# Shift and scale of a modulation as TensorE products with one moving column, in a hybrid state-space and attention layer

## The chip, the core and the metric

The kernel runs on one core of a Trainium2 chip. The metric is the device time of one execution in microseconds (us). The kernel computes in float32; its large products use the float32r form of TensorE on operands that are split in two parts.

## The reference

Only the beginning of the layer matters here. The conditioning vector `c` (1024 numbers) makes a shift, a scale and a gate for each of the 1024 channels; the tokens (2048 rows of 1024 channels) are normalized, scaled and shifted, and projected by `w_in`:

```python
c_act = jax.nn.silu(c)
mod = c_act @ w_ada[l] + b_ada[l]                # (1, 3072), w_ada is 1024 x 3072
shift, scale, gate = jnp.split(mod, 3, axis=-1)
u = _layer_norm(h) * (1.0 + scale[:, None, :]) + shift[:, None, :]
proj = u @ w_in[l]                               # 1024 x 5128: x_ssm first, then z, q, k, v, ...
```

After that come a state-space branch, an attention branch, a gated merge, an output projection and a last layer norm.

## The kernel before

All instructions are issued through small wrappers (`pe`, `dve`, `act`, `pool`, `sp`), so that the profile puts nearly all of them on line L209, and groups are told apart by the names of tiles. The order of the instructions is decided when the kernel is built: every part of the work is a Python generator (a stream), and `Model.merge` emits from the first stream whose next step would not wait by a rough clock of the engines, whose costs are in `Model.cost`. At run time each engine works its own list strictly in that order.

The first stage, called the prologue here, handles the first window of 512 tokens. Its streams are these.

- `modulation` forms shift and scale in eight steps `kt`, each for 128 channels of both. A step's weights come in a tile `wada` of 128x8x256 (two transfers, 1 MB), from a ring of four such tiles; step `kt` lets the load for `kt + 4` go. With `cact` = silu(c) as eight columns, VectorE (DVE) makes a weighted sum `acc` of six of the eight blocks (one product, five multiply-adds, 128x256 each); ScalarE (ACT) weights the other two into `pr`, and GpSimd (POOL) adds those.
- `modulation_columns` sums `acc` and `pr` over the partitions: TensorE (PE) multiplies them by the identity into a bank `bg`, 128x128 at a time, DVE reduces the 256 columns to two and adds the bias; the result is two columns of `mods`.
- `normalized` and `modulated` make the normalized tokens `xt`, transpose them on PE into a bank `pt` (four 128x128 transposes for each `kt`), and ACT makes `u` (float32) and `uh` (its rounding) from `pt` and `mods`. `low_parts` makes `ul` = `u` - `uh`. There are two `pt` banks.
- `first_weights` splits the rows `wk` of `w_in` into `hi` and `lo`.
- `phase_1a` multiplies: for each `kt` and each of four column tiles, three products of 128x512 (`uh,hi`, `ul,hi`, `uh,lo`) into banks `pp`; 96 for the first window. Then come early keys (tiles `wke`) and the next windows.

Of the kernel before, what the change touches and what calls it, by code (L numbers as in the profile page):

```python
# [16 lines left out]
S = 2048  # L17
D = 1024
NW = 4          # token windows of 512
WT = 512  # L20
KD = D // 128
NG = 32         # state-space groups
GH = 16         # channels of a group
CL = 8          # tokens of a chunk
NCH = S // CL   # chunks
CW = WT // CL   # chunks of a window
# [10 lines left out]
PKN = 163       # of a group: Bbar 16 | swapped 16 | C 16 | swapped 16 | tables 64 | powers 19 | A^7..A^0 16  # L37
# [4 lines left out]
class Model:  # L42
    """A rough clock of the engines, by which the order of emission is chosen (it computes no data)."""

    # from the end of an instruction to the start, on another engine (or the same), of one that needs it
# [34 lines left out]
    def deps(self, e, kw):  # L80
        """When the operands are there for engine e (whose own accesses are in order)."""
        rd, wt = self.aps(kw)
        r = 0.0
        for n in rd:
            if n in self.wr:
                end, by = self.wr[n]
                r = max(r, end + self.lat(e, by))
            for h in self.held:
                if n in h[2]:           # (a transfer that is still to come)
                    r = max(r, max(h[0] + 1100, self.t["sp"] + 1100, self.t["dma"]) + 1700)  # L90
# [8 lines left out]
    def cost(self, e, op, kw):  # L99
# [4 lines left out]
        if e == "pe":  # L104
            if op == "transpose":
                return n * 0.835
            if kw["rhs"].dtype == F32R:
                return max(n, 2) * (0.4167 if n >= 256 else 1.667)
            return max(n * 1.667, 60.0)
# [24 lines left out]
    def run(self, e, op, kw):  # L134
# [11 lines left out]
        for n in wt:  # L146
            # parts of a tile that transfers fill do not wait for each other
# [3 lines left out]
    def settle(self, rd, wt, dma=False):  # L151
        """Emit what is held and has to come before a read of rd and a write of wt (transfers may fill parts of a
        tile in any order)."""
# [14 lines left out]
    def merge(self, streams):  # L168
        """Emit from the first stream whose next step would not wait; streams come in order of rank."""
# [27 lines left out]
class Engine:  # L197
    """An engine whose instructions the model sees."""
# [14 lines left out]
    def when(self, **kw):  # L213
        """When an instruction with these operands could start."""
# [3 lines left out]
    def soon(self, op, /, **kw):  # L218
        """A stream's step: the instruction, emitted once it would not wait."""
        yield self.when(**kw)  # L220
        getattr(self, op)(**kw)

    def later(self, op, /, **kw):
        """The instruction, emitted once its operands are there (the streams go on meanwhile)."""
# [6 lines left out]
def hybrid_layer(ctx: ExitStack, tc: tile.TileContext, x, c, w_ada, b_ada, w_in, b_f, lam_re, lam_im,  # L231
# [32 lines left out]
    def pround(o, i):  # L264
        """Pool's copy into float32r (its rounding)."""
# [19 lines left out]
    # maskb[q, k] = 0 where k <= q, NEG elsewhere  # L285
# [4 lines left out]
    # ------------------------------------------------------------------ phase 1: input projection  # L290
    esl = ExitStack()               # left: until the projection is done
# [11 lines left out]
    def ps_tile(n=[0]):  # L303
        """One of four banks, which attention later has for scores (three) and outputs."""
# [7 lines left out]
    def bg_tile(n=None):  # L312
        if n is not None and n % 4 > 1:         # (the banks of the transposes, once attention is done)
# [6 lines left out]
    def bank():  # L320
        """Whichever of the two banks of bg_tile is free."""
# [12 lines left out]
    def split_wide(raw, n):  # L334
        """A stream that splits a chunk of weights; the tiles are there at once."""
# [8 lines left out]
    def rstd_of(p, mv, n):  # L344
        """1 / sqrt(var + eps) of the variances mv[:, :, 1]."""
# [21 lines left out]
    def until(f):  # L367
        """A condition to wait on, whatever the time."""
        return lambda: 0.0 if f() else None

    def modulation():
        """shift | 1 + scale of silu(c) @ w_ada + b_ada, as columns, 128 channels at a time."""
# [3 lines left out]
        act.activation(out=one, in_=ident[:, 0:1], func=AF.Sqrt)    # (its table is there when the layer norm needs it)  # L376
        dve.tensor_scalar(out=cth, in0=cth, scalar1=1.0, scalar2=0.5, op0=ALU.add, op1=ALU.mult)
        dve.tensor_mul(out=cact, in0=cact, in1=cth)
        prs = []

        def products(kt):
            wt = wts[kt]
            pr = T(adp, [128, 2, 256], F32, tag="pr", bufs=2, name="pr")
            for i in range(2):
                yield from act.soon("activation", out=pr[:, i], in_=wt[:, 6 + i], func=AF.Identity,
                                    scale=cact[:, 6 + i:7 + i])
            yield from pool.soon("tensor_add", out=pr[:, 0], in0=pr[:, 0], in1=pr[:, 1])
            prs.append(pr)

        yield until(lambda: units)  # L390
# [5 lines left out]
        yield from products(0)  # L396
        for kt in range(KD):
            wt = wts[kt]
            acc = T(adp, [128, 256], F32, tag="acc", bufs=2, name="acc")
            yield from dve.soon("tensor_scalar", out=acc, in0=wt[:, 0], scalar1=cact[:, 0:1], scalar2=None,  # L400
                                op0=ALU.mult)
            for k in range(1, 6):
                dve.scalar_tensor_tensor(out=acc, in0=wt[:, k], scalar=cact[:, k:k + 1], in1=acc, op0=ALU.mult,
                                         op1=ALU.add)
            if kt + 1 < KD:
                yield from products(kt + 1)
# [9 lines left out]
            accs.append((acc, prs.pop(0)[:, 0]))  # L416

    accs, ek = [], []

    def early_keys():  # L420
        """Two column tiles of the keys' weights, with which the first window goes on while the next one comes."""
# [7 lines left out]
    def modulation_columns():  # L429
        """Sums over the partitions, as columns."""  # L430
        m2 = mods.rearrange("p (a k) -> p a k", k=KD)
        b2 = bt.rearrange("p (a k) -> p a k", k=KD)
        for kt in range(KD):
            yield until(lambda: accs)
            ab = accs.pop(0)
            ps = bg_tile()
            yield pe.when(out=ps, a=ab[0], b=ab[1])
            for i in range(2):
                c = slice(i * 128, (i + 1) * 128)
                for j in range(2):  # L440
                    pe.matmul(out=ps[:, c], lhsT=ab[j][:, c], rhs=ident, start=(j == 0), stop=(j == 1))
            o = m2[:, 0:2, kt]
            yield from dve.soon("tensor_reduce", out=o, in_=ps[:, 0:256].rearrange("p (a b) -> p a b", b=128),
                                axis=AX.X, op=ALU.add)
            dve.tensor_add(out=o, in0=o, in1=b2[:, 0:2, kt])
            done["mods"] = kt + 1

    def column_sums(acc, n, c0):
        """mods[:, c0:] = sums of acc over its partitions, as columns, + b_ada."""
# [34 lines left out]
    def normalized():  # L484
        """Windows of tokens, less their mean and over their spread."""
# [21 lines left out]
    def modulated():  # L507
        """u = normalized * (1 + scale) + shift, channels on partitions."""
# [28 lines left out]
    def low_parts():  # L537
        """The two parts of u."""
        for n in range(32):
# [4 lines left out]
            yield from (pool if w == 0 or kt % 2 else dve).soon("tensor_sub", out=ul[w][kt], in0=ut, in1=f32(uh[w][kt]))  # L544
# [17 lines left out]
    def products_of(ps, w, hi, lo, c0):  # L562
        """A tile of columns of the projection of a window."""
# [7 lines left out]
    def store_parts(kind, m, w, ps):  # L571
        """Queries (scaled) or keys, in two parts."""
# [1218 lines left out]
```

## Time and profile before

| What | Value |
|---|---|
| three runs | 1916.01, 1917.6, 1920.11 us; median 1917.6 us |
| profiled execution: span of its trace, the only time that the page gives of it | 1913.3 us |
| PE busy (matmul) / weight loads | 96% / 82% of the span |
| DVE, ACT, POOL busy | 57%, 41%, 48% |
| DMA, mean over the span | 132 GB/s |

The span goes from the first to the last instruction on the chip; the 4.3 us between it and the median lie around it. A busy PE counts the time from a matmul's start to the modelled end of its last column, so that matmuls which follow each other overlap, and their distance from start to start, not their duration, says what each one takes.

### The profile page before, as it was taken

To read this page: it belongs to the slowest core of one execution; us is meant where nothing else is said; L and a number is where in the kernel's file an instruction comes from. 1 tells how busy PE (TensorE), PEld (TensorE's weight loads), DVE (VectorE), ACT (ScalarE), POOL (GpSimd) and SP (SyncE) were. 2 spreads that over 40 slices of the span, in tenths; PEclk is the share of its full clock that TensorE was granted. 3 is DMA by queue.
4 is the path that set the end of the run, shared out by engine and by line. 5 is a ranking of instruction groups with operands and counts; after the bars stand their busy time and mean duration, and the time that the engine had idled before them with its cause. 6 is when DMAs were issued, how large, how long until landed. Compare 5 with 4: busy or idle time off the path is not lost. (4 is left out here: it accounts for less than half of the span.)

```text
span 1913.3 us, 30538 instructions
## 1 busy us (share of the span) xinstructions
PE 1833.8 (96%) x10104; PEld 1565.5 (82%) x10104; DVE 1082.5 (57%) x2886; ACT 775.1 (41%) x1849; POOL 923.6 (48%) x1343
## 2 busy tenths in 40 slices
PE   4999999998999999999998999999999999899997
PEld 3789988886787888888887888988889888788886
DVE  8651114734555555552004777876777866567666
ACT  5441111121433444443114767876767866311110
POOL 5222111113889999995306566376543436533110
PEclk9899999998999999999998999999999999999999
DMA  9434346654333333335217365265364543744432
GB/s 302 138 86 119 94 110 183 149 133 121 101 94 105 100 105 97 105 101 138 91 50 189 98 169 140 77 183 152 113 201 131 151 137 127 260 146 136 131 123 89
DMA packets 276915, 252.37 MB, mean 132 GB/s; under 512 B 66396, under 2 KB 211828, under 8 KB 276756
## 3 DMA queue, kind: packets, MB, share of 16 engines
q1 hardware_dynamic: 276756, 250.41, 45.7%
q8 instruction: 80, 1.31, 0.3%
q14 instruction: 79, 0.65, 0.1%
HBM read 159.50 MB, written 86.63 MB: 129 GB/s over the span
## 5 line engine op out<-in xcount | busy, mean ns | idle before, releaser
L209 PE MATMUL pp<-uh,hi 128*128 128x512 f32 x1136 | 451.0, 397 | 0.0
L209 PE MATMUL pp<-uh,lo 128*128 128x512 f32 x1136 | 446.0, 393 | 0.0
L209 PE MATMUL pp<-ul,hi 128*128 128x512 f32 x1136 | 445.1, 392 | 0.0
L209 ACT ACTIVATE st<-pp 128x512 f32<-128x512 f32 (+2 forms) x168 | 93.9, 559 | 439.1 <-PE pp L209 383.4
L209 DVE TENSOR_TENSOR pl<-pt,ph 128x512 fp32r<-128x512 f32 (+1 forms) x288 | 183.3, 657 | 122.3 <-ACT ph L209 121.7
L209 PEld LDWEIGHTS pp<-uh,lo 128*128 128x128 f32 x1136 | 214.2, 189 | 46.3
L209 PEld LDWEIGHTS pp<-uh,hi 128*128 128x128 f32 x1136 | 216.4, 190 | 41.5
L209 PEld LDWEIGHTS pp<-ul,hi 128*128 128x128 f32 x1136 | 214.7, 189 | 41.9
L209 ACT ACTIVATE srow<-srow,nm 128x512 f32<-128x512 f32 (+2 forms) x320 | 207.6, 653 | 0.4 <-DVE nm L209 0.3
L209 ACT ACTIVATE ph<-pt 128x512 fp32r<-128x512 f32 (+1 forms) x288 | 159.8, 572 | 64.4 <-PE pt L209 51.6
L209 DVE CUSTOM_DVE_ANT_0 srow<-sc,fb 128x512 f32<-128x512 f32 (+3 forms) x288 | 163.0, 594 | 21.9 <-PE sc L209 21.9
L209 PE MATMUL sc<-ks,qd 128*128 128x512 f32 (+2 forms) x640 | 163.7, 381 | 7.1 <-DMA qd<-q_sc 7.1
L209 PE MATMUL pt<-ident,srow 128*128 128x128 f32 x1088 | 159.3, 275 | 8.7 <-DVE pl L209 4.7
L209 PE MATMUL acc<-ph,vs 128*128 128x256 f32 x576 | 163.0, 308 | 2.5 <-POOL ph L209 2.5
L209 POOL TENSOR_TENSOR oo<-oo 64x256 f32<-64x256 f32 x128 | 93.7, 732 | 143.0 <-ACT oo L209 140.0
L209 POOL TENSOR_SCALAR hi<-raw 128x512 fp32r<-128x512 f32 x60 | 39.9, 665 | 237.8 <-PE pp L209 191.7
L209 PEld LDWEIGHTS pt<-ident,srow 128*128 128x128 f32 x1088 | 128.4, 141 | 27.2 <-DVE pl L209 9.5
L209 PE MATMUL acc<-pl,vs 128*128 128x256 f32 x576 | 147.4, 282 | 0.5 <-DVE pl L209 0.5
L209 PE MATMUL bg<-bh,wh 128*128 128x512 f32 (+1 forms) x384 | 140.2, 365 | 5.1 <-DVE zt L209 5.1
L209 PE MATMUL bg<-bh,wl 128*128 128x512 f32 (+1 forms) x384 | 138.1, 360 | 0.0
L209 PE MATMUL bg<-bl,wh 128*128 128x512 f32 (+1 forms) x384 | 137.8, 359 | 0.0
L209 PEld LDWEIGHTS sc<-ks,qd 128*128 128x128 f32 x640 | 107.9, 193 | 24.4 <-issue 8.4
(240 smaller groups left out, 3811.3 us busy)
## 6 DMA issues: line engine op xcount, KB each, us to landing
xt<-in_x_dram SPq DMA_DIRECT2D x32, 512.0 KB, 3.7
qd<-q_sc SPq DMA_DIRECT2D x64, 256.0 KB, 5.4
raw<-in_w_in_dram SPq DMA_DIRECT2D x30, 512.0 KB, 4.5
wada<-in_w_ada_dram SPq DMA_DIRECT2D x16, 512.0 KB, 7.0
k_sc<-st SPq DMA_DIRECT2D x32, 256.0 KB, 3.3
v_sc<-st SPq DMA_DIRECT2D x32, 256.0 KB, 2.3
q_sc<-st SPq DMA_DIRECT2D x16, 512.0 KB, 3.3
gs_sc<-st SPq DMA_DIRECT2D x32, 256.0 KB, 2.3
```

Of the source, the lines that this page charges most:

```text
L209: return fn(kw["out"], 0.0) if op == "memset" else fn(**kw)
```

## The change

The weighted sums leave DVE, ACT and POOL. Each 128x128 block of a `wada` tile becomes the weights of a float32 matmul, and one column of `cact` (128x1) is the moving operand; eight such products add up in one column of the bank `bg`, so that a step `kt` is sixteen matmuls, and DVE adds the bias straight from `bg`. `modulation_columns` goes. `modulation` no longer waits until the first tokens are normalized. The model takes at least 110 ns instead of 60 for a float32 matmul, and for the first window the `ul` subtractions go to DVE, where they were on POOL. Comments and docstrings are dropped as well.

```diff
@@ class Model: cost
-            return max(n * 1.667, 60.0)
+            return max(n * 1.667, 110.0)
@@ modulation
-        prs = []
-
-        def products(kt):
-            wt = wts[kt]
-            pr = T(adp, [128, 2, 256], F32, tag="pr", bufs=2, name="pr")
-            for i in range(2):
-                yield from act.soon("activation", out=pr[:, i], in_=wt[:, 6 + i], func=AF.Identity,
-                                    scale=cact[:, 6 + i:7 + i])
-            yield from pool.soon("tensor_add", out=pr[:, 0], in0=pr[:, 0], in1=pr[:, 1])
-            prs.append(pr)
-
-        yield until(lambda: units)
         ps = bg_tile()
         yield pe.when(out=ps, in_=braw)
         pe.transpose(out=ps[:, 0:24], in_=braw, identity=ident[0:24, 0:24])
         dve.tensor_copy(out=bt, in_=ps[:, 0:24])
         dve.tensor_scalar(out=bt[:, 8:16], in0=bt[:, 8:16], scalar1=1.0, scalar2=None, op0=ALU.add)
-        yield from products(0)
+        m2 = mods.rearrange("p (a k) -> p a k", k=KD)
+        b2 = bt.rearrange("p (a k) -> p a k", k=KD)
         for kt in range(KD):
             wt = wts[kt]
-            acc = T(adp, [128, 256], F32, tag="acc", bufs=2, name="acc")
-            yield from dve.soon("tensor_scalar", out=acc, in0=wt[:, 0], scalar1=cact[:, 0:1], scalar2=None,
-                                op0=ALU.mult)
-            for k in range(1, 6):
-                dve.scalar_tensor_tensor(out=acc, in0=wt[:, k], scalar=cact[:, k:k + 1], in1=acc, op0=ALU.mult,
-                                         op1=ALU.add)
-            if kt + 1 < KD:
-                yield from products(kt + 1)
+            ps = bg_tile()
+            yield pe.when(out=ps, a=wt, b=cact)
+            for i in range(2):
+                for k in range(KD):
+                    pe.matmul(out=ps[:, i:i + 1], lhsT=wt[:, k, i * 128:(i + 1) * 128], rhs=cact[:, k:k + 1],
+                              start=(k == 0), stop=(k == KD - 1))
             if kt + 4 < KD:
                 load_ada(kt + 4)
...
-            accs.append((acc, prs.pop(0)[:, 0]))
+            yield from dve.soon("tensor_add", out=m2[:, 0:2, kt], in0=ps[:, 0:2], in1=b2[:, 0:2, kt])
+            done["mods"] = kt + 1
@@ modulation_columns (whole)
-            for i in range(2):
-                c = slice(i * 128, (i + 1) * 128)
-                for j in range(2):
-                    pe.matmul(out=ps[:, c], lhsT=ab[j][:, c], rhs=ident, start=(j == 0), stop=(j == 1))
-            o = m2[:, 0:2, kt]
-            yield from dve.soon("tensor_reduce", out=o, in_=ps[:, 0:256].rearrange("p (a b) -> p a b", b=128),
-                                axis=AX.X, op=ALU.add)
-            dve.tensor_add(out=o, in0=o, in1=b2[:, 0:2, kt])
-            done["mods"] = kt + 1
@@ low_parts
-            yield from (pool if w == 0 or kt % 2 else dve).soon("tensor_sub", out=ul[w][kt], in0=ut, in1=f32(uh[w][kt]))
+            yield from (pool if w and kt % 2 else dve).soon("tensor_sub", out=ul[w][kt], in0=ut, in1=f32(uh[w][kt]))
@@ hybrid_layer
-    M.merge([normalized(), modulation_columns(), modulation(), low_parts(), first_weights(), early_keys(), modulated(), phase_1a()])
+    M.merge([normalized(), modulation(), low_parts(), first_weights(), early_keys(), modulated(), phase_1a()])
```

PE's list changes in the prologue. Before, it begins as follows; the names are the bank, then the moving tile and the weights.

```order
L209 MATMUL bg<-ident,braw 128x24
L209 MATMUL pt<-ident,xt 128x128 x4
L209 MATMUL bg<-ident,acc 128x128
L209 MATMUL bg<-ident,pr 128x128
L209 MATMUL bg<-ident,acc 128x128
L209 MATMUL bg<-ident,pr 128x128
```

With the change it begins like this.

```order
L209 MATMUL bg<-ident,braw 128x24
L209 MATMUL bg<-cact,wada 128x1 x16
L209 MATMUL pt<-ident,xt 128x128 x8
L209 MATMUL bg<-cact,wada 128x1 x16
L209 MATMUL pt<-ident,xt 128x128 x4
L209 MATMUL pp<-uh_0_84,hi 128x512
L209 MATMUL pp<-ul_0_100,hi 128x512
L209 MATMUL pp<-uh_0_84,lo 128x512
```

A block of sixteen one-column products stands ahead of the first transposes, and a second one ahead of the first products `pp`. Further on, between two blocks, PE's list has this pattern, up to the eighth block (here from the third to the fourth).

```order
L209 MATMUL bg<-cact,wada 128x1 x16
L209 MATMUL pp<-uh_0_84,hi 128x512
L209 MATMUL pp<-ul_0_100,hi 128x512
L209 MATMUL pp<-uh_0_84,lo 128x512
L209 MATMUL pt<-ident,xt 128x128 x4
L209 MATMUL pp<-uh_0_84,hi 128x512
L209 MATMUL pp<-ul_0_100,hi 128x512
L209 MATMUL pp<-uh_0_84,lo 128x512
L209 MATMUL bg<-cact,wada 128x1 x16
```

So six `pp` products stand between two blocks, 36 of the window's 96 come before the eighth block, and 60 after it. After the first three windows of tokens the lists of all engines are the same as before but for the numbers of buffers.

On SP, which issues the transfers, the list before has these rows from the last two `wada` tiles on; `xt` are the tokens of the second window.

```order
L209 DMA wada<-in_w_ada_dram 128x8x128 x2
L209 DMA wke<-in_w_in_dram 128x8x256
L209 DMA xt<-in_x_dram 128x1024 x2
L209 DMA xt_404<-in_x_dram 128x1024
L209 DMA xt_405<-in_x_dram 128x1024
```

With the change these are the rows.

```order
L209 DMA wada<-in_w_ada_dram 128x8x128 x2
L209 DMA wk<-in_w_in_dram 128x512
L209 DMA xt<-in_x_dram 128x1024 x2
L209 DMA xt_394<-in_x_dram 128x1024
L209 DMA xt_395<-in_x_dram 128x1024
L209 DMA wke<-in_w_in_dram 128x8x256
```

The tokens of the second window go ahead of the early keys' weights; the `wada` transfers keep their places.

## Rows read from the trace of the kernel before

**Rows 1.** The page: span, and busy time of PE and of its weight loads.

```profile
span 1913.3 us, 30538 instructions
PE 1833.8 (96%) x10104; PEld 1565.5 (82%) x10104; DVE 1082.5 (57%) x2886; ACT 775.1 (41%) x1849; POOL 923.6 (48%) x1343
```

**Rows 2.** Stretches of 5 us: length, busy us (instructions) by engine, PEclk, DMA share, GB/s.

```profile
30.00:35.00 5.00, 5.00 (x27) 4.14 (x27) 4.51 (x9) 3.43 (x9) 4.09 (x5) 1.00 1.16 317
40.00:45.00 5.00, 3.30 (x21) 2.56 (x21) 4.82 (x8) 4.25 (x10) 3.68 (x4) 1.00 1.16 311
45.00:50.00 5.00, 2.56 (x10) 1.57 (x8) 4.82 (x6) 2.68 (x6) 5.00 (x7) 0.57 1.05 397
50.00:55.00 5.00, 4.18 (x15) 3.39 (x15) 4.82 (x8) 1.96 (x3) 3.39 (x3) 0.50 0.23 91
55.00:60.00 5.00, 4.27 (x17) 3.82 (x18) 3.80 (x9) 2.18 (x4) 2.25 (x2) 0.56 0.00 0
60.00:65.00 5.00, 5.00 (x23) 4.07 (x22) 4.83 (x13) 1.83 (x4) 2.10 (x2) 1.00 0.93 341
```

**Rows 3.** Groups of instructions of the first 90 us: busy us, mean ns, idle before.

```profile
L209 DVE SCALAR_TENSOR_TENSOR acc<-wada,cact,acc 128x256 f32<-128x256 f32 x40 | 30.7, 768 | 1.4
...
L209 POOL TENSOR_TENSOR ul<-u,uh 128x512 fp32r<-128x512 f32 x9 | 12.0, 1336 | 32.8 <-DVE uh L209 21.6 <-ACT uh L209 11.2
...
L209 DVE TENSOR_SCALAR acc<-wada,cact 128x256 f32<-128x256 f32 x8 | 5.7, 706 | 0.3 <-issue 0.3
...
L209 DVE TENSOR_TENSOR ul<-u,uh 128x512 fp32r<-128x512 f32 x2 | 1.3, 638 | 0.0
```

**Rows 4.** Timeline (start us, us): ACT waits for the second and the fourth `wada`.

```profile
17.20 0.91 ACT L209 ACTIVATE pr<-wada,cact 128x256 f32<-128x256 f32 x2 [0.70 <-DMA wada<-in_w_ada_dram]
...
25.86 0.91 ACT L209 ACTIVATE pr<-wada,cact 128x256 f32<-128x256 f32 x2 [1.08 <-DMA wada<-in_w_ada_dram]
```

**Rows 5.** Timeline: the eighth and last pair of columns of `mods`.

```profile
58.27 0.78 DVE L209 TENSOR_TENSOR mods<-mods,bt 128x2 f32<-128x2 f32 x1
```

**Rows 6.** Timeline of PE and its weight loads: float32 pairs, and transposes of 32 columns.

```profile
19.25 0.63 PE L209 MATMUL bg<-ident,pr 128*128 128x128 f32 x2
...
19.68 0.63 PE L209 MATMUL bg<-ident,acc 128*128 128x128 f32 x2
...
33.88 0.39 PE L209 MATMUL bg<-ident,pr 128*128 128x128 f32 x2
...
34.10 0.39 PE L209 MATMUL bg<-ident,acc 128*128 128x128 f32 x2
...
386.74 0.82 PEld L209 LDWEIGHTS pt<-ident,Qp 32*128 32x128 f32 x12 [0.35 <-issue]
```

**Rows 7.** Views by tile, weight loads: ns min/median/max, first and last start, form.

```profile
L209 PEld LDWEIGHTS bg<-ident,acc x4: 187/191/192, 33.6 to 34.1; 128*128 128x128 f32 x4
...
L209 PEld LDWEIGHTS bg<-CA,pkg x62: 92/94/96, 482.2 to 867.0; 128*16 128x16 f32 x62
...
L209 PEld LDWEIGHTS pt<-ident,Qp x21: 133/137/140, 386.7 to 391.7; 32*128 32x128 f32 x21
```

**Rows 8.** Timeline of PE: transposes, and products of the first window up to its end.

```profile
24.56 1.91 PE L209 MATMUL pt<-ident,xt 128*128 128x128 f32 x8
...
31.18 0.63 PE L209 MATMUL pp<-ul,hi 128*128 128x512 f32 x1
...
31.60 0.60 PE L209 MATMUL pp<-uh,lo 128*128 128x512 f32 x1
...
34.55 0.60 PE L209 MATMUL pt<-ident,xt 128*128 128x128 f32 x4
...
72.50 0.39 PE L209 MATMUL pp<-uh,lo 128*128 128x512 f32 x1
...
72.73 0.39 PE L209 MATMUL pp<-uh,wke 128*128 128x512 f32 x1
```

**Rows 9.** PE's groups between 13 and 59.4 us, one of the three `pp` kinds.

```profile
L209 PE MATMUL pp<-uh,hi 128*128 128x512 f32 x13 | 6.9, 529 | 0.0
```

More of the change, by code (lines that the diff above doesn't have):

```diff
@@ L415, in modulation @@
                 ek.append(T(adp, [128, KD, 256], F32R, tag="wada", bufs=4, name="wke"))
-            accs.append((acc, prs.pop(0)[:, 0]))
-    accs, ek = [], []
+            yield from dve.soon("tensor_add", out=m2[:, 0:2, kt], in0=ps[:, 0:2], in1=b2[:, 0:2, kt])
+            done["mods"] = kt + 1
+    ek = []
     def early_keys():
@@ L427, in early_keys @@
         done["ek"] = True
[L429 to L437, printed above, removed]
-            for i in range(2):
-                c = slice(i * 128, (i + 1) * 128)
-                for j in range(2):
-                    pe.matmul(out=ps[:, c], lhsT=ab[j][:, c], rhs=ident, start=(j == 0), stop=(j == 1))
-            o = m2[:, 0:2, kt]
-            yield from dve.soon("tensor_reduce", out=o, in_=ps[:, 0:256].rearrange("p (a b) -> p a b", b=128),
-                                axis=AX.X, op=ALU.add)
-            dve.tensor_add(out=o, in0=o, in1=b2[:, 0:2, kt])
-            done["mods"] = kt + 1
     def column_sums(acc, n, c0):
```

## The prediction

> **What bounds the kernel now.** I read the page first: PE is busy for 96% of the span [rows 1], so work taken from another engine pays only where PE waits. Then I cut the beginning into stretches of 5 us and looked for idle PE [rows 2]: it works 3.30 of 5 us from 40 to 45, 2.56 from 45 to 50, and from 60 on all of it. DVE is busy 4.82 of 5 us through 40 to 55, and the DMA share, 1.16 at 30 to 45, falls to nothing by 55. So the transfers had ended while DVE was still at work: DVE bounds the prologue.
>
> The groups say with what [rows 3]: 40 multiply-adds and 8 products on `wada`, 30.7 + 5.7 = 36.4 us. ACT waits for the second and the fourth `wada` at 17.20 and 25.86 us [rows 4], so a step's weights (with a `wk`) land every 4.33 us; the first pair is then there at 12.9 and, if the queue stays full, the eighth at 25.86 + 4 x 4.33 = 43.2 (estimates). The eighth pair of `mods` is ready only at 58.27 + 0.78 = 59.05 us [rows 5], 16 us later.
>
> Third, TensorE's clock. PEclk reads 1.00 at 30 to 35 [rows 2], but the rows there come in two kinds: two halves of a float32 product are 0.43 us apart from the next two at 19.25 and 0.22 at 33.88 [rows 6], a `pp` product takes 0.42 at 31.18 and 0.23 at 72.50 [rows 8]. That is 1.2 and then 2.4 GHz. By the means of 0.57 and 0.56 [rows 2] the clock falls near 45.7, after the half idle stretch, and rises near 59.4, in a stretch with PE at work for 4.27 us. The stretch before has 4.18 us of work and stays at 0.50. Work of some 4 us is thus sometimes enough and sometimes not.
>
> My yardstick is the end of the first window's 96 `pp` products, the start of the first `wke` product: 72.73 us [rows 8]. From there PE has no idle time for a long while and its later list is unchanged, so a shift of this point is a shift of the whole. When `mods` is complete, near 59.4, 13 products of each of the three kinds are done, 39 of 96 [rows 9], much as the 36 that will stand ahead of the last block: the race is for the date of `mods`. I add it to the median, 1917.6; the profiled execution's span, 1913.3 [rows 1], lies 4.3 below and moves alike.
>
> **The change part by part.** *Removed.* DVE's 36.4 us, the reductions, ACT's and POOL's part in the sums: all bought only the dates of `mods`. On PE, 64 half products of 128 columns go (each float32 matmul shows as two rows, with two weight loads).
>
> *Added.* 8 x 16 = 128 float32 matmuls with one moving column, 256 halves, each with a load of 128x128 weights. The trace has no float32 matmul with few columns. Below stand transposes with 32 columns: 12 loads in 0.82 us, of which one takes 0.137, so (0.82 - 0.137) / 11 = 0.062 us each [rows 6, 7]. Above stands the pair of 128 columns: (34.10 - 33.88) / 2 = 0.11 us a half, and 0.215 at 1.2 GHz [rows 6]. I take the upper end, since the load sets it: outside transposes a load of 128 columns takes 191 ns and one of 16 takes 94 [rows 7], 0.87 ns a column, 111 ns for 128; the transposes' loads are of the faster sort, 137 ns. One moving column leaves nothing to hide such a load behind. A block of 16 matmuls is then 32 x 0.1125 = 3.6 us at 2.4 GHz, 32 x 0.215 = 6.9 us at 1.2; eight blocks are 29 or 55 us, against 64 x 0.1125 = 7.2 us removed.
>
> *Moved.* Blocks stand in PE's list ahead of the transposes and `pp` products, and PE works strictly in order: between two blocks there are four transposes (0.11 or 0.215 us each) and six `pp` (0.23 or 0.42), so 1.8 or 3.4 us. DVE's add waits for its block, and behind it stands that step's `ul`, which needs it anyhow. `ul` on DVE takes 0.64 us where POOL took 1.34 [rows 3], hidden: DVE is now nearly empty. On SP the second window's tokens pass the early keys; those keys are used only from the yardstick on, and behind 2 MB of tokens their 1 MB takes, at the 397 GB/s of 45 to 50 [rows 2], till about 52 us (an estimate), so it is hidden. The floor of 110 ns in the model sets only the order shown.
>
> *The sum, at 1.2 GHz.* First block from 13.0 to 19.9; eight transposes to 21.6; second block to 28.5; four transposes and six `pp` to 31.9; third block to 38.8; five more rounds of 3.4 + 6.9 = 10.3 end the eighth block at 90.0; the 60 `pp` that are left, dense and at 2.4 GHz, 13.8 us: 103.8, which is 31 us later than 72.7. Each round at 2.4 GHz instead takes 5.4 and saves 4.8. No row shows what one-column matmuls do to the clock, since the array takes in one column where loads take 111 ns; I liken them to idle time, after which the clock fell at 45.7. The 3.4 us of dense work in a round may raise it now and then, as above: I give that one round of the six. 31 - 4.8 = 26, so 1917.6 + 26 = **1944 us**.
>
> **The rivals.** *The clock comes up* and stays, because PE has no gap from 13 us on. First block half at 1.2 (16 x 0.215 + 16 x 0.1125 = 5.2): 18.2; transposes 0.9; block 3.6: 22.7; transposes and `pp` 1.8, third block 3.6: 28.1; five rounds of 5.4: 55.1; then 13.8: 68.9. That is 3.8 us early, 1913.8: the edge of no change, since about 0.2% (3.8 us) is what a measurement of this kernel can tell. For it: the clock rose twice in dense work. Against it: the 4.18 us at 0.50 [rows 2]. The Trainium skill, page "TensorE: Matmul & The Clock Gate", section "Why this matters for your kernels", advises to keep TensorE continuously busy to reach its full rate; by that rule blocks without gaps would give this rival's time, and the trace agrees at 59.4 and not at 50 to 55.
>
> *Cheap loads*, the case on the faster side: a half costs the transposes' 0.062 us, a block 2.0, and the clock is up. A round of 2.0 + 1.8 is then shorter than the 4.33 between landings, the weights' arrival bounds, and the eighth block ends at 43.2 + 2.0; 13.8 more make 59.0, 13.7 us early: 1904. It decides from 0.079 us a half on ((4.33 - 1.8) / 32). Against it stand the 191 and 94 ns. The same page, section "Weight-path perf modes — Fast Weight Load (FWL) and DoubleRow", excludes float32 weights from the fast load; by it the sum keeps 0.1125, and the 191 ns agree.
>
> *Clock up in most rounds*, four or five of six: 31 - 4.5 x 4.8 = 9 us late, 1927.
>
> **How the numbers follow.** Low clock with none to three rounds up: 0.58, from 1934 to 1949, and to 1953 if the first `pp` after the last block are slow too (some 8 at 0.2 more) and the runs spread by the 2.5 us that they show. Clock up in most rounds 0.08. Clock up throughout 0.28, spread by some 4 us around 1914: 0.12 faster, 0.14 no change, 0.02 slower. Cheap loads 0.06. Most rounds up: 0.02 no change, 0.06 slower. Faster by over 0.2%: 0.12 + 0.06 = 0.18; within: 0.14 + 0.02 = 0.16; slower: 0.58 + 0.06 + 0.02 = 0.66. The range that holds 8 in 10 takes in both clocks: 1912 to 1953. That of the likeliest case alone is 1934 to 1953.
>
> **What would show it.** `bg<-cact,wada`: start to start of halves 0.11 (2.4 GHz) or 0.215 (1.2), against 0.06 in the cheap case. Granted clock: 0.5 in most stretches up to the last block; if 1.00 from 20 us on, the first rival. The eighth add into `mods` near 85 to 90 us (55 or 45 in the rivals), the first `wke` product near 99. ACT and DVE should wait for PE there, and PE for nobody: if PE waits for `uh` or `wada`, my picture of a PE-bound prologue is wrong. From then on each stretch should look as before, only later.

## The result, and the profile after

The changed kernel takes 1946.98 us (median of four executions, 1943.97 to 1947.41), the kernel before beside it 1918.86 (four, 1916.01 to 1921.13): the ratio is 1.0138, with a 95% interval of 1.0121 to 1.0154. It is slower by 28 us; the prediction was 1944, slower by 26. That closeness is partly luck: two terms were off by some 7 us each, in opposite directions, and a later set of executions of the same kernel gave 1957.8.

The page of the profile after begins as follows.

```profile
span 1945.6 us, 30824 instructions
PE 1873.8 (96%) x10296; PEld 1605.0 (82%) x10296; DVE 1050.3 (54%) x2838; ACT 767.9 (39%) x1833; POOL 907.4 (47%) x1327
```

Against [rows 1] DVE has 32 us less to do and the kernel is slower; PE has 40 us more, in 192 more rows. These are the stretches of 5 us that answer to [rows 2] (length, busy us and instructions of PE, PEld, DVE, ACT and POOL, then PEclk, DMA share, GB/s).

```profile
40.00:45.00 5.00, 5.00 (x35) 4.60 (x34) 0.45 (x2) 1.76 (x4) 0.00 (x0) 0.78 0.46 128
45.00:50.00 5.00, 5.00 (x38) 4.77 (x36) 0.41 (x1) 0.29 (x1) 1.61 (x2) 0.84 1.12 342
50.00:55.00 5.00, 5.00 (x28) 4.39 (x27) 0.86 (x2) 2.06 (x4) 1.62 (x2) 0.70 1.03 394
55.00:60.00 5.00, 5.00 (x27) 4.51 (x27) 0.85 (x2) 2.06 (x4) 0.64 (x1) 0.64 0.41 131
60.00:65.00 5.00, 5.00 (x25) 4.81 (x23) 0.00 (x0) 0.00 (x0) 1.00 (x2) 0.50 0.00 0
...
95.00:100.00 5.00, 3.16 (x18) 2.56 (x19) 3.27 (x8) 3.22 (x5) 1.27 (x1) 1.00 0.89 217
```

The picture of [rows 2] is turned round. From 40 to 60 us DVE, 4.82 of 5 us busy before in most of them, now does 0.41 to 0.86; PE, half idle before, is busy all the time up to 90 us. And yet PEclk reads 0.50 to 0.84 up to 65 us: PE is not idle there and runs at 1.2 GHz for much of the time. The timeline of PE shows where (start us, us, the row's form, xcount; a block of sixteen products is one row of x32, and the row behind it says where it ended).

```profile
13.38 6.99 PE L209 MATMUL bg<-cact,wada 128*128 128x1 f32 x32
20.23 1.95 PE L209 MATMUL pt<-ident,xt 128*128 128x128 f32 x8
...
32.10 3.83 PE L209 MATMUL bg<-cact,wada 128*128 128x1 f32 x32
35.80 0.66 PE L209 MATMUL pp<-uh,hi 128*128 128x512 f32 x1
...
39.24 3.71 PE L209 MATMUL bg<-cact,wada 128*128 128x1 f32 x32
...
60.66 6.82 PE L209 MATMUL bg<-cact,wada 128*128 128x1 f32 x32
67.34 0.77 PE L209 MATMUL pp<-uh,hi 128*128 128x512 f32 x1
...
70.90 6.82 PE L209 MATMUL bg<-cact,wada 128*128 128x1 f32 x32
77.58 0.77 PE L209 MATMUL pp<-uh,hi 128*128 128x512 f32 x1
```

The first block takes 20.23 - 13.38 = 6.85 us, or 0.214 us a half; the third 3.70, or 0.116. Four of the eight blocks (at 32.10, 39.24, 46.28 and 53.28) are of the short sort, four of the long. The rounds (a block and the transposes and products up to the next one) tell more: from one long block to the next it is 70.90 - 60.66 = 10.24 us, and from a short one to the next 39.24 - 32.10 = 7.14. The clock rose near the beginning of such a block and was down again near its end, so the block is short and little else; nearly all transposes and `pp` products between blocks stay at 1.2 GHz in either case. The view by tile gives the durations (ns, least, median, most).

```profile
L209 PEld LDWEIGHTS bg<-cact,wada x256: 187/331/337, 13.4 to 77.3; 128*128 128x128 f32 x128
L209 PE MATMUL bg<-cact,wada x256: 164/352/373, 13.4 to 77.4; 128*128 128x1 f32 x128
```

A load of 128 columns takes 187 ns at least, as in [rows 7], and 331 in the median, since most ran at 1.2 GHz. The last pair of `mods`, in DVE's timeline, comes 19 us later than in [rows 5]:

```profile
77.75 0.16 DVE L209 TENSOR_TENSOR mods<-bg,bt 128x2 f32<-128x2 f32 x1 [6.96 <-PE bg L209]
```

DVE had waited 6.96 us for PE. Behind that come the 60 `pp` products that are left, and at the end something new. These are rows of PE's timeline again, with the idle time before a row and what ended it in brackets.

```profile
82.84 0.63 PE L209 MATMUL pp<-uh,hi 128*128 128x512 f32 x1
83.27 0.60 PE L209 MATMUL pp<-ul,hi 128*128 128x512 f32 x1
...
84.18 0.39 PE L209 MATMUL pp<-ul,hi 128*128 128x512 f32 x1
84.41 0.40 PE L209 MATMUL pp<-uh,lo 128*128 128x512 f32 x1
...
94.40 0.49 PE L209 MATMUL pt<-ident,xt 128*128 128x128 f32 x3
96.41 0.76 PE L209 MATMUL pt<-ident,xt 128*128 128x128 f32 x5 [1.52 <-ACT xt L209]
97.60 0.66 PE L209 MATMUL pt<-ident,xt 128*128 128x128 f32 x4 [0.43 <-ACT u L209]
98.01 0.48 PE L209 MATMUL pp<-uh,wke 128*128 128x512 f32 x1
```

The first 14 of them, from 77.58 to 83.27, are some 0.43 us apart; the clock comes up near 83.7, and then they are 0.23 apart. Then PE stands still for 1.52 and 0.43 us for the second window's tokens, and the yardstick of the prediction, the first `wke` product, comes at 98.01; it was at 72.73 in [rows 8]. ACT's timeline says why the tokens are late.

```profile
87.20 1.23 ACT L209 ACTIVATE xt<-xt,nm,rs 128x1024 f32<-128x1024 f32 x1
92.50 0.60 ACT L209 ACTIVATE st<-pp 128x512 f32<-128x512 f32 x1 [4.07 <-PE pp L209]
92.99 1.24 ACT L209 ACTIVATE xt<-xt,nm,rs 128x1024 f32<-128x1024 f32 x1
94.12 0.59 ACT L209 ACTIVATE st<-pp 128x512 f32<-128x512 f32 x1
```

In ACT's list an eviction `st` stands between the second and the third `xt`; it waits 4.07 us for PE to finish a bank, and the third and fourth `xt` wait with it.

### The profile page after: what moved, and what is told of

Read it like the earlier page. It is cut to its first block, busy times and chain, and to the rows that moved or that the text cites. A ratio compares the mean times of both kernels' runs of the same rounds, so it can differ in the third digit from the quotient of the medians.

```text
span 1945.6 us, 30824 instructions
## 1 busy us (share of the span) xinstructions
PE 1873.8 (96%) x10296; PEld 1605.0 (82%) x10296; DVE 1050.3 (54%) x2838; ACT 767.9 (39%) x1833; POOL 907.4 (47%) x1327
```

## The experiments

Every comparison is with the kernel before, run beside it on the same chip; the experiments ran on three chips (numbers 8, 10 and 12), and that of the first result is not known. The theory: PE's blocks are priced by their weight loads, and by a clock that single moving columns leave at 1.2 GHz. The rivals: the float32 loads, or the columns, cost more in themselves; the order or the other parts of the change are to blame.

**128 columns instead of one.** The same products, with silu(c) spread over 128 equal columns.

```diff
+        cw = adp.tile([128, KD, 128], F32, name="cw")
+        dve.tensor_scalar(out=cw, in0=cact.unsqueeze(2).to_broadcast([128, KD, 128]), scalar1=1.0, scalar2=None, op0=ALU.mult)
-                    pe.matmul(out=ps[:, i:i + 1], lhsT=wt[:, k, i * 128:(i + 1) * 128], rhs=cact[:, k:k + 1],
+                    pe.matmul(out=ps[:, i * 128:(i + 1) * 128], lhsT=wt[:, k, i * 128:(i + 1) * 128], rhs=cw[:, k, :],
```

> The blocks of w_ada stay the weights, in the same 128 float32 matmuls, but the moving operand is 128 equal columns (silu(c) spread out once by VectorE) where the change has one. Theory: the price of a half is its weight load, 0.112 us at 2.4 GHz and 0.2135 at 1.2, with one column or 128; what the single column costs beyond that is the clock, which the changed kernel's trace shows at 0.50 in most stretches up to 83 us. With 128 columns the clock then comes up by the second or third block and stays; blocks take 3.6 to 3.7 us, the eighth add into mods comes near 55 us, the first wke product between 70 and 78, and the time is 1914 to 1924 us, some 25 us under the changed kernel. Rival 1: the float32 loads themselves, or the chain of halves into one bank, hold the clock down; then it stays at 0.50 as now, with 1943 to 1950 us. Rival 2: 128 columns lengthen a half (columns and load add up, near 0.165 us at 2.4 GHz); then blocks take 5.3 us even at the full clock and the time is some 12 us above the theory's, 1928 to 1936.

Measured: 1925.02 us, ratio 1.003 (1.0016 to 1.0043). These are rows of PE's timeline.

```profile
14.43 5.21 PE L211 MATMUL bg<-cw,wada 128*128 128x128 f32 x32 [1.07 <-DVE cw L211]
19.48 0.60 PE L211 MATMUL pt<-ident,xt 128*128 128x128 f32 x4
...
47.36 3.73 PE L211 MATMUL bg<-cw,wada 128*128 128x128 f32 x32
50.85 0.48 PE L211 MATMUL pp<-uh,hi 128*128 128x512 f32 x1
...
72.25 0.77 PE L211 MATMUL pt<-ident,xt 128*128 128x128 f32 x5 [1.51 <-ACT xt L211]
73.45 0.66 PE L211 MATMUL pt<-ident,xt 128*128 128x128 f32 x4 [0.43 <-ACT u L211]
73.86 0.48 PE L211 MATMUL pp<-uh,wke 128*128 128x512 f32 x1
```

With 128 times the columns a half is cheaper, not dearer: 3.49 us a block, 0.109 a half. The clock rose within the first block, near 17.5 us, and stays up through the prologue. Both rivals fall: neither the float32 loads nor the chain of halves into one bank hold the clock down, and 128 columns do not lengthen a half. What the single column cost beyond this is 1946.98 - 1925.02 = 22 us, worked out from two sets of runs; against the later, slower set of the changed kernel (below) it is 33. The time lies 1 us above what was expected; the wait for `xt` is here too, and the first block starts 1 us later for `cw`.

**One product of eight.** Each step forms its sums from `k = 0` alone; seven eighths of the sum are left out.

```diff
-                for k in range(KD):
-                    pe.matmul(out=ps[:, i:i + 1], lhsT=wt[:, k, i * 128:(i + 1) * 128], rhs=cact[:, k:k + 1],
-                              start=(k == 0), stop=(k == KD - 1))
+                pe.matmul(out=ps[:, i:i + 1], lhsT=wt[:, 0, i * 128:(i + 1) * 128], rhs=cact[:, 0:1],
+                          start=True, stop=True)
```

> Each step forms its two columns from one of the eight products only (k = 0), so seven eighths of the sum are left out and the numbers that follow are others; transfers, adds and all later work stay. TensorE's part in the modulation is then 2 matmuls a step in place of 16. Theory: the loss of the changed kernel is TensorE's time for the blocks, at a low clock; without it the arrival of the weights is the bound, the eighth add into mods comes near 45 us, the first wke product near 60, and the time is 1904 to 1910 us, faster than before by 0.4 to 0.7%. Rival: freed of the blocks, the first window runs into something else that is late (the second window's normalized tokens, for which TensorE already waited 1.52 + 0.43 us at 96 to 98 in the changed kernel, or the low clock in the gaps between arrivals); then 1913 to 1918 us, no better than before.

Measured: 1905.46 us, ratio 0.9929 (0.9911 to 0.9947). In PE's timeline the last block waits for its weights.

```profile
44.25 0.38 PE L209 MATMUL bg<-cact,wada 128*128 128x1 f32 x2 [1.31 <-DMA wada<-in_w_ada_dram]
...
53.76 0.50 PE L209 MATMUL pp<-uh,wke 128*128 128x512 f32 x1 [2.62 <-ACT wke L209]
```

So the weights are there by 44.2 us, and what stands between the changed kernel and 1905 us is PE's time for its blocks and the low clock that goes with them. At this yardstick that is 19 us less than in [rows 8]; the next bounds behind it (here `wke`) give part back, and by 453 us 13 of the 19 are left.

**Two parts undone.** The `ul` subtractions back on POOL, and the planner's floor of 60 ns back.

```diff
-            yield from (pool if w and kt % 2 else dve).soon("tensor_sub", out=ul[w][kt], in0=ut, in1=f32(uh[w][kt]))
+            yield from (pool if w == 0 or kt % 2 else dve).soon("tensor_sub", out=ul[w][kt], in0=ut, in1=f32(uh[w][kt]))
```

> One part of the change is undone: the ul subtractions of the first window go back to POOL. Theory: they are hidden behind TensorE's blocks on either engine (0.64 us on VectorE, 1.34 on POOL, one to every 7 to 10 us), so the time is that of the changed kernel within 4 us, 1943 to 1951. Rival: VectorE's list is what makes the second window's tokens late (the waits of TensorE at 96 to 98 us and the 2 us there); then those waits go and the time is 3 to 5 us less, 1941 to 1944.

```diff
-            return max(n * 1.667, 110.0)
+            return max(n * 1.667, 60.0)
```

> One part of the change is undone: the planner's floor for a float32 matmul is 60 ns again, as before the change, which sets nothing but the order in which instructions are listed (nine pp products between two blocks in the place of six). Theory: the sum of work up to the eighth block grows by 3 products a round, the work behind it shrinks by the same, and only the clock in the rounds may change; the longer dense stretch raises it at least as often. So within 6 us of the changed kernel, 1941 to 1950. Rival: the loss comes from the order (mods late because of it); then 10 us or more away from the changed kernel, either way.

Measured: 1948.54 us, ratio 1.0145 (1.012 to 1.0169), and 1952.97, ratio 1.0176 (1.0155 to 1.0196). Neither part is where the 28 us come from. More can't be read from these two: their single executions spread from 1941.01 to 1952.35 and from 1949.88 to 1958.56, wider than the differences asked for. The second one is 3 us above what was expected; in its profile more `pp` products stand ahead of the eighth block (52 are done when the eighth `mods` come, where the changed kernel has 37), and PE then waits four times for `xt` between 93 and 100 us, the longest time 2.65 us, after which PEclk reads 0.51 from 100 to 105.

**Earlier normalization, in vain.** This was meant to remove the wait for `xt`.

```diff
-            yield until(lambda: len(xq) >= 4 and done["mods"] >= (0, 7, 8, 8)[w])
+            yield until(lambda: len(xq) >= 4 and done["mods"] >= (0, 5, 8, 8)[w])
```

> The changed kernel, with one line of its planner other: the second window's normalization may be listed from the fifth pair of mods on, where it had to come after the seventh. TensorE's products stay as they are. Theory: the waits of TensorE for the second window's xt and u (1.52 + 0.43 us and some more between 90 and 98 us, busy 4.89 and 3.16 of 5) come from where the normalization stands in the lists of VectorE and ACT; listed earlier it is done under the blocks, the waits go, the shift of the first wke product falls from 25.3 to about 22, and the time is 1942 to 1946 us. Rival: the second window's tokens themselves land late, or the low clock fills the time that is won; then the shift stays at 25 and the time at 1945 to 1949.

Measured: 1958.35 us, with executions of 1958.7, 1961.87, 1957.99 and 1937.09; ratio 1.0173 (1.0125 to 1.022). The edit moved nothing: this condition was not what held the normalization, and the lists of all engines are those of the changed kernel. The same instructions thus took 1937 and 1962 us, on one chip. So the changed kernel was run again as it is.

> The changed kernel again, not altered, in more executions. The run with the earlier normalization turned out to hold the very same lists of instructions on all engines as the changed kernel, and yet its profile shows 1.2 GHz from the first block to 95.9 us, while the changed kernel's own profile shows four of its eight blocks at 2.4. Theory: with one moving column the clock in the rounds is a matter of when its rise happens to fall, so the same program has a spread, from about 1937 us (clock up in most rounds) to 1962 (in none), and the executions here lie spread over more than 8 us in that range. Rival: the clock repeats itself from execution to execution on one chip; then the times lie within 4 us of each other, near 1946 or near 1959.

Measured: 1957.78 us (five executions, 1957.45 to 1960.38), ratio 1.0198 (1.0184 to 1.0212). The theory's spread within a set did not show; the rival came out, a clock that repeats itself, within 3 us and near 1959. But the set lies 11 us above the first one (this set ran on another chip than the 1937 and 1962 above, and the chip of the first is not known), and the set before it had 1937 beside 1958 on one chip, so the repetition is no rule either. This is PE's timeline.

```profile
72.97 6.82 PE L209 MATMUL bg<-cact,wada 128*128 128x1 f32 x32
...
83.21 6.82 PE L209 MATMUL bg<-cact,wada 128*128 128x1 f32 x32
...
89.89 0.77 PE L209 MATMUL pp<-uh,hi 128*128 128x512 f32 x1
...
108.44 0.76 PE L209 MATMUL pt<-ident,xt 128*128 128x128 f32 x5 [1.52 <-ACT xt L209]
...
110.05 0.48 PE L209 MATMUL pp<-uh,wke 128*128 128x512 f32 x1
```

Here all eight blocks are long, from the third on 10.24 us from one to the next, and the eighth ends at 89.89: the prediction's sum for 1.2 GHz throughout says 90.0. (In this profile, as in that of the kernel before, the column PEclk prints 1.00 ahead of the first change of clock that was recorded, at 95.5 us; the blocks' 6.82 us show that the clock was at 1.2 GHz. The spacing of equal rows is the safer reading.)

**Operands swapped.** A column of silu(c) as weights, 256 columns of `w_ada` moving; the row of sums is then turned into columns.

```diff
-            for i in range(2):
-                for k in range(KD):
-                    pe.matmul(out=ps[:, i:i + 1], lhsT=wt[:, k, i * 128:(i + 1) * 128], rhs=cact[:, k:k + 1],
-                              start=(k == 0), stop=(k == KD - 1))
+            for k in range(KD):
+                pe.matmul(out=ps[0:1, 0:256], lhsT=cact[:, k:k + 1], rhs=wt[:, k, :], start=(k == 0), stop=(k == KD - 1))
+            yield from dve.soon("tensor_copy", out=row, in_=ps[0:1, 0:256])
+            for i in range(2):
+                pe.matmul(out=ps[:, 256 + i:257 + i], lhsT=row[:, i * 128:(i + 1) * 128], rhs=ident[0:1, 0:1],
+                          start=True, stop=True)
```

> The operands of the changed kernel's products are swapped: a column of silu(c) becomes the weights (128x1) and the 256 columns of a w_ada row block the moving operand, 8 float32 matmuls a step in the place of 16; the row of 256 sums is copied by VectorE and turned into two columns by two products with one row. Theory 1 (moving columns set the clock): the 16 halves of a step take about 0.215 us each at 2.4 GHz (256 columns, twice the 0.112 that 128 columns take), 3.4 us a step, the clock comes up in the third step at the latest and stays, and the time is near that of the run with 128 equal columns, 1916 to 1928 us. Rival 1: the clock follows how much of the array is at work, and one column of weights leaves it low as one moving column does; then 6.9 us a step and 1940 to 1955. Rival 2: the longer way from product to mods (copy, turn) makes TensorE wait in every step, 1930 to 1940 at the full clock.

Measured: 1921.58 us, ratio 1.0004 (0.9992 to 1.0015), as before the change. The view by tile:

```profile
L209 PEld LDWEIGHTS bg<-wada,cact x128: 79/84/128, 13.3 to 60.5; 128*1 128x1 f32 x128
L209 PE MATMUL bg<-wada,cact x128: 377/379/634, 13.4 to 60.7; 128*1 128x256 f32 x128
```

These are rows of PE's timeline, the second step and the row behind it.

```profile
20.76 3.61 PE L209 MATMUL bg<-wada,cact 128*1 128x256 f32 x16
24.31 0.66 PE L209 MATMUL pt<-ident,xt 128*128 128x128 f32 x4
```

A load of one column takes 84 ns in the median, well under the spacing of the halves; the matmuls' median of 379 ns and largest of 634 tell that nearly all ran at 2.4 GHz. A step of 16 halves takes 3.55 us (20.76 to 24.31), 0.222 a half, as expected. With columns moving, the clock is up from 19 us on, though only one column of weights is at work: rival 1 falls. Rival 2 falls too: PE is busy 5.00 of 5 us in each stretch from 15 to 75. (The profile is of the slowest of the ten executions, 1926.16 us.)

**The wait for the tokens, at a steady clock.** The run with 128 columns, with the second window's tokens loaded one step earlier.

```diff
+            if kt == 3:
+                for i in range(4, 8):
+                    load_x(i)
             if kt == 4:
...
-                for i in range(4, 8):
-                    load_x(i)
-            yield until(lambda: len(xq) >= 4 and done["mods"] >= (0, 7, 8, 8)[w])
+            yield until(lambda: len(xq) >= 4 and done["mods"] >= (0, 5, 8, 8)[w])
```

> The run with 128 equal moving columns (steady clock), with the second window's tokens loaded one w_ada tile earlier and their normalization allowed from the fifth pair of mods on; this time the lists do change: VectorE has the statistics of these tokens two steps earlier, ACT has two of the four normalizations ahead of the last u. Theory: the rest of that run's loss, the first wke product at 73.86 in the place of 70 to 72, is TensorE's wait for the second window's xt (1.51 + 0.43 us and what lies around them); with xt ready the wait goes, the shift of TensorE's list against before goes from +4 to between -1 and +1 us, and the time is 1919 to 1922 us. Rival: the tokens ahead of the last w_ada tile make that block late instead, and the shift stays at +4 or grows, 1924 to 1930 us.

Measured: 1924.11 us, ratio 1.0016 (1.0006 to 1.0026), against 1.003 (1.0016 to 1.0043): no difference that can be told.

```profile
14.50 6.78 PE L211 MATMUL bg<-cw,wada 128*128 128x128 f32 x32 [1.08 <-DVE cw L211]
21.11 0.60 PE L211 MATMUL pt<-ident,xt 128*128 128x128 f32 x4
...
73.62 0.66 PE L211 MATMUL pt<-ident,xt 128*128 128x128 f32 x4 [0.22 <-ACT u L211]
74.03 0.48 PE L211 MATMUL pp<-uh,wke 128*128 128x512 f32 x1
```

The wait went from 1.51 + 0.43 to 0.22 us, and yet the first `wke` product is no earlier (74.03, 73.86 there). Two other things took back what the wait gave. The first block takes 21.11 - 14.50 = 6.61 us, where it took 5.05 there, because the clock rose only near its end; and sixteen transposes of the second window stand ahead of that product, where it was twelve (some 0.4 us). So the run tells neither for the theory nor against it, and what the wait is worth by itself is not shown. The eighth `mods` come at 64.59 us in place of 56.71, as the rival said, but with 65 `pp` products begun by then where there were 38. By 453 us both runs stand 1.7 us behind the kernel before.

**A part of the sums on PE.** From the kernel before: DVE sums four blocks or five in place of six, and PE takes the others with 128 moving columns (one silu(c), the rest zero) into the bank in which it sums over the partitions; the load of a further `w_ada` tile is let go behind these products. The diff is that of one block; for two, the 5 is a 4.

```diff
-            for k in range(1, 6):
+            for k in range(1, 5):
...
+                for k in range(5, 6):
+                    pe.matmul(out=ps[:, c], lhsT=wts[kt][:, k, c], rhs=czs[0][:, k - 5], start=(k == 5), stop=False)
                 for j in range(2):
-                    pe.matmul(out=ps[:, c], lhsT=ab[j][:, c], rhs=ident, start=(j == 0), stop=(j == 1))
+                    pe.matmul(out=ps[:, c], lhsT=ab[j][:, c], rhs=ident, start=False, stop=(j == 1))
```

> From the kernel before: VectorE sums four of the eight blocks in the place of six, ACT and POOL keep their two, and the other two blocks go to TensorE as weights, with a moving operand of 128 columns of which the first is silu(c) and the others zero, so that they add up in the same bank as the sums over the partitions (8 more halves a step, 0.9 us at 2.4 GHz, 7.2 us in all). Theory: VectorE bounded the prologue with 36.4 us of sums, TensorE was half idle at 40 to 60 us; a third of the sums off VectorE (12.3 us) brings the eighth mods from 59 to about 48 us, the work of TensorE fits in its idle time, and the first wke product comes 7 to 12 us earlier: 1907 to 1914 us. Rival: the added 7.2 us of TensorE, some of it at the low clock, and the waits of its queue for VectorE's sums eat the gain; then 1915 to 1925.

> As the run that takes two blocks from VectorE, but with one block only: VectorE sums five, TensorE multiplies one (4 more halves a step, 3.6 us in all at 2.4 GHz). Theory: VectorE's sums fall by 6.1 us, the eighth mods come near 53 us, the first wke product 3 to 6 us earlier, 1911 to 1916 us, half of what two blocks give. Rival: the gain is eaten as above, 1916 to 1922.

Measured: two blocks on PE give 1916.3 us, ratio 0.9978 (0.9968 to 0.9989); one block gives 1912.02, ratio 0.9954 (0.9939 to 0.997). Both are faster than the kernel before, but the smaller step gives twice the gain, against what was expected: for two blocks the rival's time came out. These are a stretch and rows of PE's timeline from the run with one block.

```profile
45.00:50.00 5.00, 2.48 (x20) 2.29 (x21) 4.79 (x11) 3.47 (x7) 3.55 (x5) 1.00 1.04 396
```

```profile
49.56 0.49 PE L209 MATMUL bg<-ident,acc 128*128 128x128 f32 x2 [1.96 <-DVE acc L209]
...
63.05 0.39 PE L209 MATMUL pp<-uh,wke 128*128 128x512 f32 x1
```

With one block the eighth `mods` are there at 52.64 us, near the 53 expected. DVE still bounds the end (PE waits 1.96 us for `acc`), the clock stays up where it fell in [rows 2], and the yardstick comes 9.7 us earlier, where 3 to 6 were expected. With two blocks the eighth `mods` come no earlier (53.18, where 48 was expected), and only 34 `pp` products are begun by then, where the run with one block has 52. These are a row and a stretch from the run with two blocks.

```profile
24.58 0.66 PE L209 MATMUL pt<-ident,xt 128*128 128x128 f32 x4 [2.64 <-ACT uh L209]
```

```profile
25.00:30.00 5.00, 4.53 (x23) 4.04 (x21) 2.72 (x4) 3.46 (x8) 4.17 (x5) 0.66 1.16 312
```

Up to the eighth `mods` the waits that PE's timeline marks come to the same in both runs, 8.8 and 8.9 us: those for DVE's `acc` are 2.3 with two blocks and 5.9 with one, but those for ACT's `uh` are 5.0 and 1.0. Beyond one block, what DVE saves PE thus waits for elsewhere. PE has 32 more halves to do besides, 3.6 us at 0.11, and the clock of 0.66 over these 5 us takes some 1.7 us (both are estimates); the medians are 4.3 us apart. A run that takes these parts one by one was not made.

## Why the prediction was right, step by step

*DVE bounds the prologue, the weights land 16 us earlier*: right. With next to nothing on PE the last block waits for weights until 44.2 us (43.2 was estimated), and the time falls to 1905.

*The price of a half*, 0.1125 or 0.215 us set by the load of 128 columns: right. 0.209 to 0.214 at 1.2 GHz, 0.109 with the clock up, and the same within 0.003 us with one column or 128. The cheap half of 0.062 us was not seen. The Trainium skill, page "TensorE: Matmul & The Clock Gate", section "Weight-path perf modes — Fast Weight Load (FWL) and DoubleRow", which leaves float32 weights out of the fast load, agrees with the 187 ns of the quickest load here.

*The sum at 1.2 GHz, the eighth block to 90.0 us*: right to 0.1 us where the clock stayed down (89.89), rounds of 10.24 where 10.3 was said.

*One round of the six at 2.4 GHz*: this is the step that was mis-sized. In the profile on record four blocks ran at 2.4 GHz, in the later set none. And a rise gives less than the 4.8 us that were credited: it comes with the block and is gone when the block ends, so a round gets 10.24 - 7.14 = 3.1 us. Four times 3.1 is 12.4, and 90.0 - 12.4 = 77.6 is where the eighth block ended.

*Clock up in most rounds*, four or five of six, was a rival at 0.08, with 1927 us. The four short blocks lie in four of the six rounds, so the condition that came true in the profile on record is this rival's, and not that of the likeliest case (none to three). Its price was wrong: it took whole rounds at 2.4 GHz, 5.4 us each, where the transposes and products stayed at 1.2 GHz. That the time came out near 1944 all the same is luck.

*The 60 products that are left, 13.8 us*: too small by 6.6. From 77.58 to 98.01 it took 20.4 us: 14 products at some 0.43 us cost 3 us more (the prediction had this for its upper end only), twelve transposes of the second window now stand ahead of the first `wke` product (1.7 us, a term that the sum did not have), and PE waits 1.95 us. The two errors, 12.4 - 4.8 = 7.6 us one way and 6.6 the other, nearly cancel, and 98.01 came where "near 99" had been said. In the set with the clock down nothing cancels: 110.05, and 37 us over the kernel before beside it (1957.78, 1920.35). The range, whose upper end was 1953, holds the result and would not have held that set.

*PE waits for nobody there*: wrong by those 1.52 + 0.43 us. The prediction looked at the transfers of the second window's tokens alone; that their normalization stands behind `st` in ACT's list, and `st` behind PE, was not looked at. What the wait is worth by itself was not isolated: in the run at a steady clock it went, and a clock that rose later took its gain back.

*The clock comes up and stays* was the strongest rival, at 0.28, by the rule of the same page, section "Why this matters for your kernels", that a TensorE kept busy reaches its full rate. The trace disagrees as far as a busy PE in the profile counts as busy: PE works 5.00 of 5 us from 60 to 65 at 0.50. With 128 columns moving, the same matmuls in nearly the same order come near what the rival forecast: blocks of 3.5 us, the first `wke` product at 73.86 where it said 68.9 (PE's wait of 1.94 us, the twelve transposes' 1.7 and a first block that starts 1.4 us later make up that), 1925 us where it said 1914 and the kernel before beside it took 1920. So the likening of one-column matmuls to idle time held in what it forecast, a low clock in most of the prologue. Its premise, that the half idle stretch brought the clock down at 45.7, is weaker than it looks: most of the idle time of 45 to 50 lies behind the fall (PE's longest wait there, 2.71 us, ends at 50.28), and in the run with one block on PE the clock stayed up through a stretch as idle, 2.48 of 5 us at work.

*From then on as before, only later*: nearly. The shift is 25.3 us at the first `wke` product and at 162 us, 27.6 at 507 and 32.3 at the end, while the medians differ by 28.1. Some of this is the profile of before: the changed kernel's profiled execution took 1947.41 us for a span of 1945.6, so 1.8 us lie around a span, not the 4.3 read from before; that profile was a quick execution by some 2.5 us.

What stays open: why the same list met four rises of the clock in one set of executions and none in another. The section "What's actually happening" of that page says that the start of the full rate differs from run to run of one kernel; that agrees with the first rise near 32.5 us in one profile and 95.5 in the other, but no run took the reason apart, nor chip from set. Nor is it settled where the last microseconds of the runs at a steady clock go.

## What to carry to other kernels

Work moved to an idle engine must be priced on that engine's own terms: here 128 matmuls of one column each cost a full weight load, 0.11 us a half at 2.4 GHz and 0.21 at 1.2, and the clock was at 1.2 GHz for nearly all that stood between them. If such a sum is to run on TensorE, let many columns move (spread the column, or swap the operands: 22 to 25 us better here, which brought back the time of the kernel before and no more); and move only as much as the busy engine must lose, since one block of six was worth twice as much as two. Where a time hangs on the clock, run the kernel in several sets before believing a difference of some microseconds.

## What was not expected of the hardware

In these runs the clock went with the number of moving columns and not with the busy share of PE: 1.2 GHz in most stretches with one column though PE was 5.00 of 5 us busy, 2.4 GHz from 17.5 us on with 128 columns (21 in a second run) and from 19 us on with 256 columns and a single column of weights. A float32 matmul with one moving column is not cheaper than one with 128: 0.1116 us a half (39.24 to 42.81 us, 32 halves) and 0.109. And one program, with the same lists on every engine, had sets of executions at 1944 to 1947 and at 1957 to 1960 us, and in a third set one of 1937 beside three of 1958 to 1962.
